# Feed-forward up and gate products by 2x2 blocks with seven block products in six of eight row pairs, activations stationary

## The chip, the cores and the metric

One core of one Trainium2 chip runs the kernel: one launch, 256 tokens, two layers. The metric is the device time of that launch in microseconds. The engines are named as the profile names them: PE (matrix products; PEld is its weight load), DVE (vector), ACT (scalar, activations), POOL (GpSimd), SP (which issues most of the DMAs). Tensors lie in HBM; the engines work on SBUF, and PE writes its sums to the eight banks of PSUM, each 128 partitions by 512 float32.

## The reference

Two layers on x of 256 x 2048, all in float32. Each has mixers (a recurrence and pooling in the first, linear and sparse attention in the second), an output projection, and a feed-forward part. Only the feed-forward parts are touched:

```python
D_MODEL = 2048
D_FF = 4 * D_MODEL                                  # 8192
D_FF_2 = -(-8 * D_MODEL // (3 * 256)) * 256         # 5632
...
h2 = rms_norm(x, mlp_norm[i])
x = x + jnp.square(jax.nn.relu(h2 @ w_ffn_up[i])) @ w_ffn_down[i]
...
m = rms_norm_2(h, ffn_norm_g)
return h + (jax.nn.silu(m @ w_gate) * (m @ w_up)) @ w_down
```

## The kernel before

**Products.** A float32 operand is split in two tiles of a shorter format (fp32r): a high part (a rounding, by ACT) and a low part (the operand less its high part, by DVE). A product is three matmuls: high by high, high by low, low by high. Weights are split as they arrive: `load` (L231) brings 512 KB into a tile `r` (128 x 1024; the pool `raw` has 5), `stream` (L236) makes `h` with ACT at L240 and `l` with DVE at L244 (the pools `hi` and `lo` have 3 each).

**Two forms of product.** `gemm_a` (L251) holds 128 x 128 of the weights stationary and moves the 256 tokens: 16 blocks of K (the summed dimension) by three matmuls of 256 columns (L262 to L264) give one tile of 128 outputs by 256 tokens. `gemm_b_part` (L725) holds 128 x 128 of the activations stationary and moves 512 columns of weights (L740 to L742).

**Feed-forward 1** (in `block1`, L820): eight rounds. A round has an up stage (eight `gemm_a` tiles, 1024 of the 8192 hidden columns, each followed by ReLU, a square and a split) and a down stage (four column blocks of `gemm_b_part` over the round's 1024 hidden rows, added into x by DVE). **Feed-forward 2** (`ffn2`, L1331): six rounds of the same kind with a gate tile and an up tile for each 128 of the 5632 hidden columns. In all that is 64 + 88 tiles of `gemm_a`, or 19 lots of eight, and a lot covers 1024 weight columns over the whole K of 2048.

**What sets the order.** The code is written in program order. A scheduler, working from its own estimate of durations, then fixes one order of instructions per engine at compile time, and allocates each pool's slots. At run time each engine follows its order strictly, waiting on semaphores for inputs and for slots to come free. PSUM has three pools: `acc` (4 banks), `fr` (2), `ch` (2).

## Time and profile before

| | |
|---|---|
| device time, median of 3 runs | 2485.89 us (2485.54 to 2486.83) |
| span of the profiled execution, first to last instruction | 2485.7 us |
| PE busy | 2455.0 us, 99% |
| DVE busy | 1547.7 us, 62% |
| ACT busy | 1149.9 us, 46% |
| POOL busy | 217.5 us, 9% |
| mean granted PE clock, as a share of full speed | 0.993 |

The table is the profile's first part. Matmuls are pipelined: the duration of one record overlaps the next, so PE's rate is read from the distance between starts. A share over the whole span mixes stages, so the windows and timelines of single stages, below, are what the argument rests on.

### The profile page before, as it was taken

How to read it: one execution, taken by the hardware profiler on the slowest of the kernel's cores; microseconds unless marked ns; L12 is line 12 of the kernel's file. 1: busy time of each engine (PE TensorE's matmuls, PEld its weight loads, DVE VectorE, ACT ScalarE, POOL GpSimd, SP SyncE). 2: the span in 40 equal slices, each digit the busy share in tenths (PEclk: the TensorE clock that was granted, in tenths of full speed). 3: DMA queues.
4: the chain of work that ended last, by engine and by line, in shares of the span. 5: the costliest groups of instructions: out<-in, count | busy, mean ns of one | idle time of the engine just before them, and what ended most of it. 6: DMA issues, size and time to landing. Idle time of an engine off the chain costs nothing.

```text
span 2485.7 us, 40916 instructions
## 1 busy us (share of the span) xinstructions
PE 2455.0 (99%) x16396; PEld 2224.1 (89%) x16396; DVE 1547.7 (62%) x2436; ACT 1149.9 (46%) x1686; POOL 217.5 (9%) x321
## 2 busy tenths in 40 slices
PE   9999999999999999999999998999999999999999
PEld 8988888989989989988887897888989999998988
DVE  7788866555555555556674677766555555555555
ACT  5545445544444444445652466545444444444443
POOL 1543320000000000000010044200000000000000
PEclk9999999999999999999999999999999999999999
DMA  6443336555555555556556543255555655555554
GB/s 230 153 130 111 97 115 237 182 192 186 187 190 185 188 192 187 187 189 235 180 184 213 179 149 118 90 196 185 179 190 185 187 186 186 188 185 187 186 190 158
DMA packets 135406, 439.59 MB, mean 177 GB/s; under 512 B 26784, under 2 KB 29216, under 8 KB 134064
## 3 DMA queue, kind: packets, MB, share of 16 engines
q1 hardware_dynamic: 130032, 423.58, 52.1%
q10 hardware_dynamic: 5184, 13.41, 1.4%
q8 instruction: 128, 2.10, 0.3%
q14 instruction: 62, 0.51, 0.1%
HBM read 429.59 MB, written 7.34 MB: 176 GB/s over the span
## 4 chain that ended last, share of the span: by engine, by line
PE 94%; DVE 4%; ACT 1%; DMA 1%; issue 1%; POOL 0%; SPq 0%; DVEq 0%; ACTq 0%
PE acc L262 16%; PE acc L263 16%; PE acc L264 16%; PE acc L740 13%; PE acc L741 13%; PE acc L742 13%; PE ch L361 3%; PE fr L361 2%; DVE l L244 1%; PE fr L782 1%; PE acc L361 1%; PE ch L582 0%; PE ch L585 0%; DVE X L1002 0%; PE acc L375 0%
## 5 line engine op out<-in xcount | busy, mean ns | idle before, releaser
L244 DVE TENSOR_TENSOR l<-r,h 128x1024 fp32r<-128x1024 f32 x774 | 951.5, 1230 | 737.0 <-ACT h L240 728.8
L240 ACT CAST h<-r 128x1024 fp32r<-128x1024 f32 x780 | 818.8, 1050 | 1102.2 <-PE acc L742 448.1
L262 PE MATMUL acc<-qh,h 128*128 128x256 f32 x1824 | 520.8, 286 | 0.0
L264 PE MATMUL acc<-qh,l 128*128 128x256 f32 x1824 | 519.3, 285 | 0.0
L263 PE MATMUL acc<-ql,h 128*128 128x256 f32 x1824 | 519.2, 285 | 0.0
L264 PE MATMUL acc<-xh,l 128*128 128x256 f32 x1536 | 439.0, 286 | 0.5 <-DVE l L244 0.5
L262 PE MATMUL acc<-xh,h 128*128 128x256 f32 x1536 | 439.4, 286 | 0.0
L263 PE MATMUL acc<-xl,h 128*128 128x256 f32 x1536 | 438.6, 286 | 0.0
L262 PEld LDWEIGHTS acc<-qh,h 128*128 128x128 f32 x1824 | 350.5, 192 | 4.0 <-issue 3.5
L263 PEld LDWEIGHTS acc<-ql,h 128*128 128x128 f32 x1824 | 350.5, 192 | 1.7 <-issue 1.2
L264 PEld LDWEIGHTS acc<-qh,l 128*128 128x128 f32 x1824 | 350.2, 192 | 1.1 <-issue 0.9
L741 PE MATMUL acc<-l,qh 128*128 128x512 f32 x768 | 300.4, 391 | 0.0
L742 PE MATMUL acc<-h,ql 128*128 128x512 f32 x768 | 299.3, 390 | 0.0
L263 PEld LDWEIGHTS acc<-xl,h 128*128 128x128 f32 x1536 | 295.8, 193 | 2.7 <-issue 1.3
L262 PEld LDWEIGHTS acc<-xh,h 128*128 128x128 f32 x1536 | 295.6, 193 | 2.8 <-issue 0.9
L264 PEld LDWEIGHTS acc<-xh,l 128*128 128x128 f32 x1536 | 295.7, 193 | 2.5 <-DVE l L244 0.7
L740 PE MATMUL acc<-h,qh 128*128 128x512 f32 x768 | 275.2, 392 | 0.0
L741 PE MATMUL acc<-l,xh 128*128 128x512 f32 x608 | 237.2, 390 | 0.0
L742 PE MATMUL acc<-h,xl 128*128 128x512 f32 x608 | 236.3, 389 | 0.0
L740 PE MATMUL acc<-h,xh 128*128 128x512 f32 x608 | 214.7, 390 | 0.0
L740 PEld LDWEIGHTS acc<-h,qh 128*128 128x128 f32 x768 | 144.0, 188 | 30.8 <-issue 1.2
L741 PEld LDWEIGHTS acc<-l,qh 128*128 128x128 f32 x768 | 144.2, 188 | 29.9 <-issue 0.4
(413 smaller groups left out, 2418.4 us busy)
## 6 DMA issues: line engine op xcount, KB each, us to landing
r<-w_ffn_up SPq DMA_DIRECT2D x128, 512.0 KB, 3.3
r<-w_ffn_down SPq DMA_DIRECT2D x128, 512.0 KB, 3.4
r<-w_gate SPq DMA_DIRECT2D x88, 512.0 KB, 3.9
r<-w_up SPq DMA_DIRECT2D x88, 512.0 KB, 3.5
r<-w_down SPq DMA_DIRECT2D x88, 512.0 KB, 4.2
r<-w_in SPq DMA_DIRECT2D x70, 512.0 KB, 3.4
r<-w_out SPq DMA_DIRECT2D x64, 512.0 KB, 3.3
r<-w_in_2a SPq DMA_DIRECT2D x58, 512.0 KB, 3.3
```

The costliest lines, as they stand in the source:

```text
L240: nc.scalar.copy(h, r)
L244: eng.tensor_sub(l, r, h.bitcast(F32))
L262: nc.tensor.matmul(o, wh, xh, start=k == 0, stop=False)
L263: nc.tensor.matmul(o, wh, xl, start=False, stop=False)
L264: nc.tensor.matmul(o, wl, xh, start=False, stop=k == n - 1)
L361: self.nc.tensor.matmul(out, lhsT, rhs, start=start, stop=stop)
L740: nc.tensor.matmul(ps[t], ah, wh, start=first and k == 0, stop=False)
L741: nc.tensor.matmul(ps[t], ah, wl, start=False, stop=False)
L742: nc.tensor.matmul(ps[t], al, wh, start=False, stop=last and k == nk - 1)
L782: nc.tensor.transpose(ps[:, o:o + 128], self.x[:, t, kk * 128:kk * 128 + 128], self.c("ident"))
```

## The change

The up and gate products no longer use `gemm_a`. A new method `group` computes 256 tokens by 1024 columns with activations stationary, and there are 8 + 11 = 19 groups, one for each lot above; in the second feed-forward part a group holds 512 gate and 512 up columns side by side. K is taken in eight row pairs of 256. A pair of rows times 1024 columns is a 2x2 problem: token halves by K blocks by column halves. Pairs 0 and 4 (`PLAIN`) make it with eight block products, the other six with seven, in Winograd's form of Strassen's scheme. A block product is three matmuls of 512 columns.

The seven products need sums of the weight blocks. Two tiles carry them: `t13` (two of the sums, made by one DVE addition) and `t24` (two more, made by two POOL additions, the second from the first). `t13`, `t24` and two plain pieces (`ra`, and the first half of `rb`) are each split into high and low. The low parts are made by DVE (`ra`, `t13`), by POOL (half of `rb`; the second half of `t24`), and the first half of `t24` by POOL in odd pairs and by DVE in even ones. A pool `more` (2 slots each) holds the parts of `rb` and `t24`, a pool `sums` (2) the sums. The sums of activations are made once, in `pair_chunk`, which takes the place of `norm_chunk` ahead of both feed-forward parts. All eight PSUM banks belong to one pool during the feed-forward parts; a group accumulates seven or eight products in eight banks over all pairs and then combines them (three ACT copies, eight DVE additions). The results have tokens on partitions, so they are transposed back by PE (`to_hidden`) for the down products. Down stages keep their matmuls (`ffn_down`). They run one round late: group 1 follows group 0 without a down stage between in the first part, and in the second part groups 1, 2, 3, 5, 7 and 9 follow a group directly.

```diff
+PLAIN = (0, 4)
...
-    a["w_ffn_up"] = lay_a(g["w_ffn_up"][0], 64)
+    a["w_ffn_up"] = lay_s(g["w_ffn_up"][0])
...
-    a["w_gate_2"] = lay_a(g["w_gate_2"][0], 44)
-    a["w_up_2"] = lay_a(g["w_up_2"][0], 44)
+    both = np.stack([g["w_gate_2"][0].reshape(D, 11, 512), g["w_up_2"][0].reshape(D, 11, 512)], 2)
+    a["w_gu_2"] = lay_s(both.reshape(D, 11 * 1024))
...
+            a12, a22, s1, s3, s2, s4, a11, a21 = (f[:, j] for j in range(8))
+            nc.vector.tensor_sub(s1, a21, a22)
+            nc.gpsimd.tensor_sub(s3, a11, a21)
+            nc.vector.tensor_sub(s2, s1, a11)
+            nc.vector.tensor_add(s4, a12, s2)
+            nc.scalar.copy(h, f[:, :7])
+            nc.vector.tensor_sub(l, f[:, :7], h.bitcast(F32))
...
+    def lows(self, r, h, eng=None):
+        l = self.low(r.shape[-1], r.shape[-1] < 1024)
+        (eng or self.nc.vector).tensor_sub(l, r, h.bitcast(F32))
+        return l
+    def low(self, n=1024, more=False):
+        return (self.more if more else self.lo).tile([128, 1024], F32R, name="l", tag="l")[:, :n]
+    def highs(self, r, more=False):
+        h = (self.more if more else self.hi).tile([128, 1024], F32R, name="h", tag="h")[:, :r.shape[-1]]
+        self.nc.scalar.copy(h, r)
+        return h
+    def three(self, ps, a, h, l, w, first, last):
+        mm = self.nc.tensor.matmul
+        ah, al = a
+        mm(ps, ah, h[:, w], start=first, stop=False)
+        mm(ps, ah, l[:, w], start=False, stop=False)
+        mm(ps, al, h[:, w], start=False, stop=last)
...
+    def group(self, w, pairs, out):
+        nc = self.nc
+        q = {}
+        turn = self.hold()
+        one, two = slice(0, 512), slice(512, 1024)
+        def add(name, a, h, l, w, first, last):
+            if first:
+                q[name] = self.bank("acc")
+            self.three(q[name], a, h, l, w, first, last)
+        start = min(i for i in range(8) if i not in PLAIN)
+        for i in range(8):
+            sh, sl = pairs[i]
+            a = [(sh[:, j], sl[:, j]) for j in range(sh.shape[1])]
+            ra = self.load(w[i, 0].rearrange("p k n -> p (k n)"))
+            rb = self.load(w[i, 1].rearrange("p k n -> p (k n)"))
+            if i in PLAIN:
+                ha = self.highs(ra)
+                la = self.lows(ra, ha)
+                hb = self.highs(rb)
+                lb = self.lows(rb, hb)
+                f = i == PLAIN[0]
+                add("8", a[1], hb, lb, two, f, False)
+                add("8", a[3], ha, la, two, False, i == PLAIN[-1])
+                add("2", a[0], ha, la, one, f, False)
+                add("2", a[2], hb, lb, one, False, False)
+                add("3", a[0], hb, lb, two, f, False)
+                add("3", a[2], ha, la, two, False, False)
+                add("4", a[1], ha, la, one, f, False)
+                add("4", a[3], hb, lb, one, False, False)
+                if i == 0:
+                    turn()
+                continue
+            a12, a22, s1, s3, s2, s4, a11 = a
+            f, e = i == start, i == 7
+            t13 = self.sums.tile([128, 1024], F32, name="t13", tag="t")
+            nc.vector.tensor_add(t13.rearrange("p (a n) -> p a n", a=2), ra.rearrange("p (a n) -> p a n", a=2),
+                                 rb[:, two].unsqueeze(1).to_broadcast([128, 2, 512]))
+            t24 = self.sums.tile([128, 1024], F32, name="t24", tag="t")
+            nc.gpsimd.tensor_add(t24[:, one], t13[:, one], ra[:, two])
+            nc.gpsimd.tensor_add(t24[:, two], t24[:, one], rb[:, one])
+            h = self.highs(ra)
+            l = self.lows(ra, h)
+            add("1", a11, h, l, one, f, e)
+            add("3", s4, h, l, two, False, e)
+            h = self.highs(rb[:, one], True)
+            l = self.lows(rb[:, one], h, nc.gpsimd)
+            add("2", a12, h, l, one, False, e)
+            h = self.highs(t13)
+            l = self.lows(t13, h)
+            add("5", s1, h, l, one, f, e)
+            add("7", s3, h, l, two, f, e)
+            h = self.highs(t24, True)
+            l = self.low(more=True)
+            (nc.gpsimd if i % 2 else nc.vector).tensor_sub(l[:, one], t24[:, one], h[:, one].bitcast(F32))
+            nc.gpsimd.tensor_sub(l[:, two], t24[:, two], h[:, two].bitcast(F32))
+            add("6", s2, h, l, one, f, e)
+            add("4", a22, h, l, two, False, e)
+        c11, c12, c21, c22 = out
+        V = nc.vector
+        tmp = lambda: self.comb.tile([128, 512], F32, name="cb", tag="cb")
+        c1, u2, u3 = tmp(), tmp(), tmp()
+        nc.scalar.copy(c22, q["8"])
+        nc.scalar.copy(c1, q["1"])
+        nc.scalar.copy(c12, q["3"])
+        V.tensor_add(c11, c1, q["2"])
+        V.tensor_add(c12, c12, q["5"])
+        V.tensor_add(c22, c22, q["5"])
+        V.tensor_add(u2, c1, q["6"])
+        V.tensor_add(u3, u2, q["7"])
+        V.tensor_add(c21, u3, q["4"])
+        V.tensor_sub(c12, c12, u2)
+        V.tensor_sub(c22, c22, u3)
...
+    def to_hidden(self, cols, hidden, j0, banks):
+        nc = self.nc
+        for k in range(0, 4, 2):
+            ps = banks[k // 2]
+            for a in range(2):
+                for t in range(2):
+                    o = a * 256 + t * 128
+                    nc.tensor.transpose(ps[:, o:o + 128], cols[t][:, (k + a) * 128:(k + a) * 128 + 128], self.c("ident"))
+            hh, hl = (x[(j0 + k) // 4][:, (j0 + k) % 4:(j0 + k) % 4 + 2].rearrange("p k t -> p (k t)") for x in hidden)
+            nc.scalar.copy(hh, ps)
+            nc.vector.tensor_sub(hl, ps, hh.bitcast(F32))
...
-        for s in range(8):
-            hh, hl = self.half_tiles()
-            for i in range(8):
-                ps = self.gemm_a(I["w_ffn_up"], s * 8 + i, act)
-                a = tp.tile([128, T], F32, name="relu", tag="relu")
-                nc.scalar.activation(a, ps, AF.Relu)
-                b = tp.tile([128, T], F32, name="relu2", tag="relu2")
-                nc.vector.tensor_mul(b, a, a)
-                self.split(hh[i], hl[i], b)
...
+        for s in range(9):
+            if s < 8:
+                c = [tp.tile([128, 512], F32, name="c", tag="c", bufs=4) for _ in range(4)]
+                self.group(I["w_ffn_up"][s], self.n_pairs, c)
+                hidden = self.hidden_quarts()
+                for n in range(2):
+                    for t in range(2):
+                        x = c[2 * t + n]
+                        nc.scalar.activation(x, x, AF.Relu)
+                        nc.scalar.activation(x, x, AF.Square)
+                    self.later.append(((c[n], c[2 + n]), hidden, 4 * n))
+                ready.append(hidden)
+            if s == 0:
...
+    def ffn_down(self, w, hidden, s, add, then=None, nk=8):
+        chunks = [(h[:, k], l[:, k]) for h, l in zip(*hidden) for k in range(4)][:nk]
+        for n in range(4):
+            ps = self.acc2()
+            turn = self.hold()
+            self.gemm_b_part(ps, w, n, chunks, s * 8, True, True)
+            turn()
+            add(n, ps)
...
-        for s in range(6):
-            nh = 8 if s < 5 else 4
-            hh, hl = (x[s % 2 * 8:s % 2 * 8 + nh] for x in hidden)
-            for i in range(nh):
-                j = s * 8 + i
-                g = tp.tile([128, T], F32, name="g", tag="g")
-                nc.vector.tensor_mul(g, self.gemm_a(I["w_gate_2"], j, act), rb)
-                nc.scalar.activation(g, g, AF.Silu)
-                u = tp.tile([128, T], F32, name="u", tag="u")
-                nc.vector.tensor_mul(u, self.gemm_a(I["w_up_2"], j, act), rb)
-                nc.vector.tensor_mul(u, u, g)
-                self.split(hh[i], hl[i], u)
...
+        for g in range(12):
+            if g < 11:
+                c = [tp.tile([128, 512], F32, name="c", tag="c", bufs=4) for _ in range(4)]
+                self.group(I["w_gu_2"][g], self.n_pairs, c)
+                if g % 2 == 0:
+                    hidden = self.hidden_big(g // 2)
+                    ready.append(hidden)
+                for t in range(2):
+                    gate, up = c[2 * t:2 * t + 2]
+                    nc.scalar.activation(gate, gate, AF.Silu, scale=r[:, t:t + 1])
+                    nc.vector.scalar_tensor_tensor(gate, up, r[:, t:t + 1], gate, ALU.mult, ALU.mult)
+                self.later.append(((c[0], c[2]), hidden, g % 2 * 4))
+            if g % 2 and g > 1 and g < 11:
+                self.ffn_down(I["w_down_2"], ready.pop(0), g // 2 - 1, self.add_x)
+        self.ffn_down(I["w_down_2"], ready.pop(0), 4, self.add_x)
+        self.ffn_down(I["w_down_2"], ready.pop(0), 5, store, nk=4)
```

How the orders change. On DVE, first a row of an up stage of the kernel before (`l` is the low part of a weight tile `r`; `relu2` a hidden tile, `ql` its low part):

```order
L244 TENSOR_TENSOR l_5994<-r_5990,h_5992 128x1024
L842 TENSOR_TENSOR relu2_5918<-relu_5916 128x256
L244 TENSOR_TENSOR l_6024<-r_6020,h_6022 128x1024
L249 TENSOR_TENSOR ql_5651<-relu2_5918,qh_5650 128x256
L244 TENSOR_TENSOR l_6061<-r_6057,h_6059 128x1024
L842 TENSOR_TENSOR relu2_5985<-relu_5983 128x256
L244 TENSOR_TENSOR l_6091<-r_6087,h_6089 128x1024
L249 TENSOR_TENSOR ql_5653<-relu2_5985,qh_5652 128x256
L244 TENSOR_TENSOR l_6128<-r_6124,h_6126 128x1024
L842 TENSOR_TENSOR relu2_6052<-relu_6050 128x256
```

and then pairs 5, 6 and 7 of a group of the changed kernel (`t13`, and the low parts `l` of `r` and of `t13`; one row makes half of the low part of a `t24`):

```order
L910 TENSOR_TENSOR t13_7108<-r_7104,r_7106 128x1024
L853 TENSOR_TENSOR l_7115<-r_7104,h_7113 128x1024
L853 TENSOR_TENSOR l_7132<-t13_7108,h_7130 128x1024
L910 TENSOR_TENSOR t13_7155<-r_7151,r_7153 128x1024
L853 TENSOR_TENSOR l_7162<-r_7151,h_7160 128x1024
L853 TENSOR_TENSOR l_7179<-t13_7155,h_7177 128x1024
L853 TENSOR_TENSOR l_7209<-r_7198,h_7207 128x1024
L910 TENSOR_TENSOR t13_7202<-r_7198,r_7200 128x1024
L928 TENSOR_TENSOR l_7189<-t24_7157,h_7187 128x512
L853 TENSOR_TENSOR l_7226<-t13_7202,h_7224 128x1024
```

Between two activation tiles DVE had two subtractions of 1024 columns for 128 output columns; now every pair of rows has an addition and two subtractions of 1024, and none of the activation's.

On POOL, before, around the first feed-forward part (the last rows of the first mixer, L902 at the end of the first layer, L1187 in the second):

```order
L651 TENSOR_TENSOR pd_4912<-pf_4914,u_4897 128x16
L620 TENSOR_TENSOR y_4131<-y_4131,bv_2811 128x256
L620 TENSOR_TENSOR y_4145<-y_4145,bv_3113 128x256
L902 TENSOR_TENSOR x_res_5089<-x_res_5089,fn_12519 128x2048 x2
L1187 MEMSET cu_15003 128x3
```

and in the changed kernel pairs 5 and 6 of the same group:

```order
L853 TENSOR_TENSOR l_7125<-r_7106,h_7123 128x512
L913 TENSOR_TENSOR t24_7110<-t13_7108,r_7104 128x512
L914 TENSOR_TENSOR t24_7110<-t24_7110,r_7106 128x512
L928 TENSOR_TENSOR l_7142<-t24_7110,h_7140 128x512
L929 TENSOR_TENSOR l_7142<-t24_7110,h_7140 128x512
L853 TENSOR_TENSOR l_7172<-r_7153,h_7170 128x512
L913 TENSOR_TENSOR t24_7157<-t13_7155,r_7151 128x512
L914 TENSOR_TENSOR t24_7157<-t24_7157,r_7153 128x512
L929 TENSOR_TENSOR l_7189<-t24_7157,h_7187 128x512
```

POOL had no instruction in the feed-forward part; it now has four or five of 512 columns in each pair of seven products, and the two that end a pair wait for ACT's rounding of `t24`.

On DVE at the passage from a down stage to a group (the first row is the last weight tile of the down stage, `x_res` its additions, then the group's pairs 0 and 1):

```order
L267 TENSOR_TENSOR l_7587<-r_7583,h_7585 128x1024
L910 TENSOR_TENSOR t13_7651<-r_7647,r_7649 128x1024
L853 TENSOR_TENSOR l_7613<-r_7607,h_7611 128x1024
L853 TENSOR_TENSOR l_7617<-r_7609,h_7615 128x1024
L1022 SCALAR_TENSOR_TENSOR x_res_5105<-acc_7527,r2_5720,x_res_5105 128x512
L1022 SCALAR_TENSOR_TENSOR x_res_5105<-acc_7528,r2_5720,x_res_5105 128x512
L853 TENSOR_TENSOR l_7658<-r_7647,h_7656 128x1024
L910 TENSOR_TENSOR t13_7702<-r_7698,r_7700 128x1024
L853 TENSOR_TENSOR l_7676<-t13_7651,h_7674 128x1024
```

The `t13` of pair 1 stands ahead of the two subtractions of pair 0, and both stand ahead of the down stage's last additions.

## Rows read from the trace of the kernel before

**Rows 1.** The page, part 1: busy time (share of the span) x instructions of each engine.

```profile
PE 2455.0 (99%) x16396; PEld 2224.1 (89%) x16396; DVE 1547.7 (62%) x2436; ACT 1149.9 (46%) x1686; POOL 217.5 (9%) x321
```

**Rows 2.** The page, part 4: the chain that ended last, by engine and line.

```profile
PE 94%; DVE 4%; ACT 1%; DMA 1%; issue 1%; POOL 0%; SPq 0%; DVEq 0%; ACTq 0%
PE acc L262 16%; PE acc L263 16%; PE acc L264 16%; PE acc L740 13%; PE acc L741 13%; PE acc L742 13%; PE ch L361 3%; PE fr L361 2%; DVE l L244 1%; PE fr L782 1%; PE acc L361 1%; PE ch L582 0%; PE ch L585 0%; DVE X L1002 0%; PE acc L375 0%
```

**Rows 3.** Windows over two up stages and the down stage between; columns in the second line.

```profile
core 0 of [0], span 2485.7 us
core 0: us, PE busy (x) PEld busy (x) DVE busy (x) ACT busy (x) POOL busy (x), PEclk, DMA share, GB/s
918.00:964.00 46.00, 46.00 (x385) 46.00 (x384) 25.35 (x32) 20.89 (x30) 0.00 (x0) 1.00 0.57 184
964.00:1007.50 43.50, 43.50 (x194) 36.03 (x193) 24.38 (x25) 17.45 (x18) 0.00 (x0) 1.00 0.61 193
1007.50:1053.50 46.00, 46.00 (x384) 45.96 (x384) 25.46 (x32) 20.88 (x30) 0.00 (x0) 1.00 0.56 184
```

**Rows 4.** Timeline of PE where a down stage passes into an up stage.

```profile
start us, us, engine line op out<-in xcount [idle before <-releaser]
...
917.26 0.39 PE L740 MATMUL acc<-h,qh 128*128 128x512 f32 x1
917.49 0.39 PE L741 MATMUL acc<-l,qh 128*128 128x512 f32 x1
917.72 0.39 PE L742 MATMUL acc<-h,ql 128*128 128x512 f32 x1
917.94 0.28 PE L262 MATMUL acc<-xh,h 128*128 128x256 f32 x1
918.06 0.28 PE L263 MATMUL acc<-xl,h 128*128 128x256 f32 x1
918.18 0.28 PE L264 MATMUL acc<-xh,l 128*128 128x256 f32 x1
```

**Rows 5.** Timeline of PE, six transposes between two matmuls of the out projection.

```profile
417.06 0.82 PE L782 MATMUL fr<-cst,x_res 128*128 128x128 f32 x6
...
417.63 0.48 PE L741 MATMUL acc<-l,qh 128*128 128x512 f32 x1
```

**Rows 6.** Groups by line: busy us, mean ns, idle before. First DVE, then ACT, then POOL.

```profile
L244 DVE TENSOR_TENSOR l<-r,h 128x1024 fp32r<-128x1024 f32 x774 | 951.5, 1230 | 737.0 <-ACT h L240 728.8 <-PE fr L361 0.5
L240 ACT CAST h<-r 128x1024 fp32r<-128x1024 f32 x780 | 818.8, 1050 | 1102.2 <-PE acc L742 448.1 <-PE acc L263 347.6 <-issue 261.6
...
L812 DVE TENSOR_TENSOR x_res<-x_res,acc 128x512 f32<-128x512 f32 x64 | 41.0, 680 | 6.2 <-PE acc L742 6.2
...
L491 POOL TENSOR_TENSOR G<-G,cst 128x512 f32<-128x512 f32 x12 | 15.6, 1302 | 14.9 <-ACT G L490 14.9
L244 POOL TENSOR_TENSOR l<-r,h 128x1024 fp32r<-128x1024 f32 x6 | 14.4, 2403 | 33.9 <-ACT h L240 31.3 <-ACT rhs L577 2.6
...
L1253 POOL TENSOR_TENSOR E<-b 128x512 f32<-128x512 f32 x7 | 8.6, 1241 | 19.7 <-DVE b L1231 7.1 <-PE fr L361 6.3 <-PE acc L264 3.3
```

**Rows 7.** Single lines, min/median/max ns: POOL L354, and DVE L1260 (both inputs in SBUF).

```profile
L354 POOL TENSOR_TENSOR d<-z x27: 612/613/1593, 38.6 to 249.3; 128x256 f32<-128x256 f32 x27
...
L1260 DVE TENSOR_TENSOR E<-E,Q x7: 673/681/1219, 1547.3 to 1586.2; 128x512 f32<-128x512 f32 x7
```

**Rows 8.** Timeline of POOL and DVE from 90 us: start us, us, engine, line.

```profile
89.54 0.73 POOL L472 TENSOR_TENSOR BKh<-sig,cum 128x256 f32<-128x256 f32 x1 [0.57 <-DVE sig L469]
...
89.71 0.41 DVE L352 TENSOR_TENSOR z<-acc,rb 128x256 f32<-128x256 f32 x1
...
90.23 0.74 POOL L475 TENSOR_TENSOR BKe<-sig,e_end 128x256 f32<-128x256 f32 x1
...
90.38 1.67 DVE L244 TENSOR_TENSOR l<-r,h 128x1024 fp32r<-128x1024 f32 x1
...
90.93 1.59 POOL L354 TENSOR_TENSOR d<-z 128x256 f32<-128x256 f32 x1
```

**Rows 9.** Timeline of DVE and POOL from 157 us.

```profile
157.63 1.22 DVE L244 TENSOR_TENSOR l<-r,h 128x1024 fp32r<-128x1024 f32 x1
...
157.76 2.25 POOL L491 TENSOR_TENSOR ql<-ql,cst 128x512 f32<-128x512 f32 x1 [1.09 <-ACT ql L490]
```

**Rows 10.** Windows in the recurrence and the second mixer, with the granted clock (PEclk).

```profile
159.80:163.20 3.40, 1.58 (x14) 1.39 (x13) 1.11 (x3) 0.82 (x2) 1.29 (x3) 1.00 0.67 164
163.20:166.60 3.40, 1.90 (x20) 1.84 (x21) 2.05 (x4) 0.36 (x1) 1.05 (x4) 0.67 0.89 206
1542.20:1545.60 3.40, 3.40 (x31) 3.40 (x30) 3.40 (x6) 3.01 (x5) 3.32 (x4) 1.00 0.02 5
1545.60:1549.00 3.40, 0.66 (x6) 0.48 (x5) 3.40 (x6) 2.23 (x3) 3.28 (x4) 1.00 0.46 157
1549.00:1552.40 3.40, 2.17 (x16) 1.87 (x14) 3.40 (x7) 2.41 (x10) 1.30 (x2) 0.67 0.00 0
```

More of the change, by code (lines that the diff above doesn't have):

```diff
@@ L364, in first_tiles @@
         nc = self.nc
-        out = [self.acc.tile([128, 512], F32, name="acc", tag="acc")[:, :T] for _ in range(n)]
+        out = [self.bank("acc")[:, :T] for _ in range(n)]
         for half in range(2):
@@ new lines, in hold, with turn @@
+    def hold(self):
+        todo, self.later = [(x, [self.bank("fr") for _ in range(2)]) for x in self.later], []
+        def turn():
+            for x, banks in todo:
+                self.to_hidden(*x, banks)
+        return turn
+    def to_hidden(self, cols, hidden, j0, banks):
+        nc = self.nc
+        for k in range(0, 4, 2):
[7 more added lines that the diff above has]
+            nc.vector.tensor_sub(hl, ps, hh.bitcast(F32))
@@ L1234, in gla_scores @@
         sc = [scA[:, :, :128], scB]
-        ps = [self.fr.tile([128, 512], F32, name="fr", tag="fr") for _ in range(2)]
+        ps = [self.bank("fr") for _ in range(2)]
         for t in range(2):
```

237 lines of the change are left out of this document (158 added, 79 removed).

## The prediction, made before the changed kernel ran

> **What bounds the kernel now.** Read the page first: PE is busy 99% of the span, DVE 62%, ACT 46%, POOL 9% [rows 1]. Then the chain that ended last: 94% of it is PE, nearly all in the two product forms [rows 2]. Then one up stage alone: for 46 us PE never stops, while DVE works 25.35, ACT 20.89 and POOL nothing [rows 3]. So the up and gate products are bound by PE's own rate, and a saving there counts in full as long as the engines that feed PE keep up. Whether they do is the question here.
>
> PE's rate is read from starts [rows 4]: 512 columns every 0.227 us (917.26, 917.49, 917.72), 256 columns every 0.120 us. A lot of eight tiles is 384 matmuls of 256 columns, 384 x 0.120 = 46.1 us, which is the window of [rows 3]; the 19 lots take 876 us. A down stage is 192 x 0.227 = 43.5 us and is not changed.
>
> **What the change takes from PE.** The order of the built kernel has 3306 matmuls of 512 columns in the groups, 174 in each: 2 pairs x 24 + 6 x 21. 174 x 0.227 = 39.4 us, 6.6 less than 46.1, and 19 x 6.64 = 126 us in all. So the change does what it says, and a version that lacks the saving is no rival. Against it stand 216 transposes. Six of them and the next matmul are 0.57 us apart [rows 5], 0.095 each. 152 of them lie in down stages, where PE is the bound: +14 us. The other 64 lie at the start of a group, where I expect PE to wait anyway: nothing, and 6 us if that cover is gone.
>
> **What it puts on DVE and POOL.** Counts are from the built order, over all 19 groups. DVE: 114 additions for t13 and 304 subtractions, 418 of 1024 columns, each with both inputs in SBUF, at 1.23 us [rows 6]; 98 of 512 columns with both inputs in SBUF (half low parts, the last two of the combination, the gate product) at 0.68 us [rows 7]; and six additions a group with one input in PSUM, also 0.68 [rows 6]. POOL: 532 operations of 512 columns, where it had none. A lone one takes 1.24 to 1.30 us, half of the one of 1024 columns with the fp32r output is 1.20 [rows 6]; I take 1.25. For one group that is DVE 22 x 1.23 + 5.2 x 0.68 = 30.6 us and POOL 28 x 1.25 = 35.0 us. Side by side either would fit under PE's 39.4.
>
> **They don't run side by side.** This is the reading on which all rests. In [rows 8] POOL's L475 starts at 90.23 and DVE's subtraction L244 at 90.38. L244 takes 1.67 us in place of 1.23: it stands until POOL is through at 90.97. POOL's next one, L354 (128x256, 0.61 us when alone, its median in [rows 7]), starts at 90.93 and takes 1.59: it stands until DVE is through at 92.05. In [rows 9] the roles are the other way: DVE starts first, takes its 1.22, and POOL's 512-column operation takes 2.25, 1.0 more than alone. L352, which reads PSUM, runs through POOL's L472 at its usual 0.41 [rows 8]. So a DVE operation with two inputs in SBUF and a POOL operation wait for each other, and those of DVE in a group are of just that kind: L244 is the very operation that the new low parts are, and t13 has two SBUF inputs as well. What is saved at a change of hands: the three of [rows 8] take 92.52 - 90.23 = 2.29 us where 0.74 + 1.23 + 0.61 = 2.58 would be the sum, so 0.14 for each of two changes.
>
> The Trainium skill has this as a rule: on "SBUF — State Buffer", section "Who interferes with whom", a DVE instruction with two SBUF inputs and a GpSimd instruction that reads SBUF exclude each other, and the later one blocks until the other has finished. The trace agrees but for the 0.14 us. By the page alone there would be no saving at the change of hands, and the low end of the sum below would be 2750 in place of 2617.
>
> **The sum for a group.** Both engines share one door, so their times add: 30.6 + 35.0 = 65.6 us a group. At best there is a saving at both ends of each of the 27 DVE operations, 27 x 2 x 0.14 = 7.6: 58.0. At worst the door is empty while POOL waits in each of six pairs for ACT to round t24 (L240's 1.05 us [rows 6]) and DVE has nothing ready: 65.6 + 6.3 = 71.9. I take 65.6, the two set against each other, since DVE's order has the next pair's work behind each of its rows but the slots (3 in lo, 2 in sums) hold it back some of the time. All three are above the 46.1 of before, so in the groups PE waits for low parts and sums; its 39.4 us lie beside them and no longer count.
>
> How much of a group's work is done before PE reaches it? During a down stage the door is half empty (DVE 24.38 of 43.5 us, POOL 0 [rows 3]). By the order and the slots, the two low parts of pair 0, the t13 of pair 1 and POOL's five operations of pair 1 can be done ahead: 3 x 1.23 + 5 x 1.25 = 9.95 us; then lo, sums and more are full. At a group's end PE still has six matmuls behind the last low part (1.4 us), while two subtractions of the combination (1.4) are not waited for: these cancel. So:
>
> - 7 groups follow a group directly: 65.6 - 46.1 = +19.5 each, +137.
> - 12 follow a down stage or an out projection: 55.6 - 46.1 = +9.5 each, +114.
> - transposes in down stages: +14.
> - where a group ends, the next stage's first two banks wait for an ACT copy and a DVE addition (0.68 [rows 6]) that stand behind low parts in DVE's order: 0 to 2 us, 1 taken, x 19 = +19.
> - PE's clock: in the groups PE works 39.4 of 55.6 to 65.6 us, 60 to 71%. In [rows 10] a window with 1.58 us busy of 3.40 is followed by one at 0.67 of the full clock, and one with 0.66 likewise; windows with 3.40 busy are not. At half speed (1.2 GHz) a pair's 21 matmuls would take twice 4.76, 9.5 us, still about what the door takes for it, so a fall is covered but where it reaches into the next stage: up to 3.4 us at half speed, 1.7 lost, x 19 = 32. I take 10.
>
> Sum: 2485.7 (the span; the median of the runs is 2485.89, the same to 0.2 us) + 137 + 114 + 14 + 19 + 10 = 2780. With 58.0 for a group: 7 x 11.9 + 12 x 2.8 + 14 = 131, 2617. With 71.9 (11 us of it ahead): 7 x 25.8 + 12 x 14.8 + 14 + 38 + 32 = 443, 2929.
>
> Costed at nothing: ACT's roundings, 22 x 1.05 + 6 of half the size, about 26 us, and under 12 us of copies and activations, in 55 to 66 us; the loads, 1 MB a pair in 9 us and more, where before it was 1 MB in 5.8 us at a DMA share of 0.57 [rows 3]; the sums of activations, 24 small operations of DVE and POOL for each feed-forward part, beside the out projection.
>
> **The rivals.**
>
> 1. *PE stays the bound, and the kernel is faster.* If the new forms do not exclude each other (t13's second input is read twice over, POOL's outputs are partly fp32r), POOL's 35.0 us plus six waits of 1.05 are 41 us a group, about PE's 39.4 plus transposes. Then the time is 2485.7 - 126 + 20 + 19 = 2399. It turns on the door's time for a group, g: 7 x (g - 46.1) + 12 x (g - 56.1) + 43 is nothing at g = 50 us, and below that the kernel is faster. Against it: in [rows 8] and [rows 9] the engines exclude each other in both directions with the same kind of operands.
>
> 2. *The door stands empty in the waits.* The two engines pass work back and forth: t13 (DVE), two additions (POOL), rounding (ACT), low parts (POOL). If DVE's strict order has nothing ready in each of these waits, the group is at 71.9 or somewhat over and the time at 2870 to 2960. For it: two slots in sums. Against it: DVE's three operations of the next pair.
>
> 3. *PE's clock stays at 1.2 GHz in the groups.* Then PE's 174 matmuls take twice 39.4, 79 us a group, PE is the bound again, and the time is 2485.7 + 19 x 32.7 + 33 = 3140. For it: [rows 10]. [...]
>
> **How the numbers follow.** The door as bound, in its own range 2617 to 2929, has 0.88, of which the upper part from 2870 (rival 2) has 0.18; rival 1 has 0.07; rival 3 has 0.04; 0.01 is left for a time within 0.2% of before, where the gain and the door's cost happen to meet. The forecast is 2780. The range of 2630 to 2930 leaves out rivals 1 and 3 and the edges. A change of 0.2% is about what a measurement of this kernel can tell from none; faster 0.07, same 0.01, slower 0.92.
>
> **What would show it.** In the changed kernel's trace: in the groups PE idle, waiting for low parts from POOL and DVE; L853, L913 and L929 on POOL at about 2.3 us where DVE works beside them, and the 1024-column operations of DVE at 1.7 to 2.4; DVE and POOL never both moving; a group of 55 to 66 us by windows, a down stage still at 43.5 to 45. I am wrong if POOL's operations stay near 1.25 us while DVE is busy (rival 1), if the granted clock in the groups is near 0.5 (rival 3), or if DVE and POOL both stand idle a good part of a group (rival 2).

## The result, and the profile after

The changed kernel takes 2790.24 us (median of 4 runs, 2785.5 to 2791.44), the kernel before 2486.34 us in the same comparison: a ratio of 1.1215, 95% interval 1.1199 to 1.1231. That is 304 us slower, inside the range and 10 us from the forecast. The profiled execution spans 2789.4 us.

The page of after, part 1 (compare [rows 1]), and the PE clock in 40 slices:

```profile
PE 2520.0 (90%) x12618; PEld 2041.0 (73%) x12618; DVE 2052.6 (74%) x2548; ACT 1362.7 (49%) x1915; POOL 1241.4 (45%) x865
...
PEclk9999999899999999999999999998889989898999
```

PE has 3778 fewer instructions and is no longer busy all the time; POOL has gone from 217.5 to 1241.4 us. Its added records take 1028 us: 532 operations, 1.93 us each, where a lone one of this size takes 1.24 to 1.30 [rows 6].

Groups by line, DVE then POOL (busy us, mean ns of one | idle before it):

```profile
L853 DVE TENSOR_TENSOR l<-r,h 128x1024 fp32r<-128x1024 f32 x190 | 367.6, 1945 | 29.6 <-ACT h L861 28.8
L853 DVE TENSOR_TENSOR l<-t,h 128x1024 fp32r<-128x1024 f32 x114 | 200.7, 1760 | 122.7 <-ACT h L861 122.7
L910 DVE TENSOR_TENSOR t<-r 128x1024 f32<-128x1024 f32 x114 | 194.1, 1703 | 62.1 <-POOL t L913 28.5 <-POOL l L929 13.1 <-DMA r<-w_ffn_up 10.9
...
L913 POOL TENSOR_TENSOR t<-t,r 128x512 f32<-128x512 f32 x114 | 242.8, 2130 | 51.5 <-DVE l L853 46.0 <-POOL l L929 4.1
L914 POOL TENSOR_TENSOR t<-t,r 128x512 f32<-128x512 f32 x114 | 240.5, 2109 | 6.5
L853 POOL TENSOR_TENSOR l<-r,h 128x512 fp32r<-128x512 f32 x114 | 215.3, 1889 | 398.3 <-ACT h L861 398.3
```

DVE's operations of 1024 columns with two SBUF inputs, 1.23 us before [rows 6], take 1.70 to 1.95 now. The timelines of POOL and DVE in one group show the two taking turns (start us, us):

```profile
2180.77 2.16 POOL L913 TENSOR_TENSOR t<-t,r 128x512 f32<-128x512 f32 x1
2182.88 2.26 POOL L853 TENSOR_TENSOR l<-r,h 128x512 fp32r<-128x512 f32 x1
2185.10 2.27 POOL L914 TENSOR_TENSOR t<-t,r 128x512 f32<-128x512 f32 x1
2188.53 2.20 POOL L928 TENSOR_TENSOR l<-t,h 128x512 fp32r<-128x512 f32 x1 [1.16 <-ACT h L861]
2190.69 1.29 POOL L929 TENSOR_TENSOR l<-t,h 128x512 fp32r<-128x512 f32 x1
2191.95 1.29 POOL L853 TENSOR_TENSOR l<-r,h 128x512 fp32r<-128x512 f32 x1
...
2179.80 1.98 DVE L853 TENSOR_TENSOR l<-t,h 128x1024 fp32r<-128x1024 f32 x1 [0.26 <-ACT h L861]
2181.70 4.52 DVE L853 TENSOR_TENSOR l<-r,h 128x1024 fp32r<-128x1024 f32 x2
2186.47 1.98 DVE L910 TENSOR_TENSOR t<-r 128x1024 f32<-128x1024 f32 x1 [0.25 <-DMA r<-w_gu]
2188.37 1.21 DVE L853 TENSOR_TENSOR l<-r,h 128x1024 fp32r<-128x1024 f32 x1
```

While DVE is at work, POOL's operations take 2.16 to 2.27; once DVE has stopped, at 2189.58, the next two take 1.29 each. DVE's pair of 4.52 us is 2.26 each. Read by where the records end, one operation ends at a time and nothing is lost between them: DVE's pair ends at 2186.22, POOL's L914 at 2187.37 (1.15 later), DVE's L910 at 2188.45 (1.08 later). So a record of 2.2 us is some 1.1 us of waiting for the other engine and some 1.1 us of work. This is [rows 8, 9] for a whole group.

Windows: a group behind a down stage and the down stage after it, then two groups that follow a group directly (columns in the first line):

```profile
core 0: us, PE busy (x) PEld busy (x) DVE busy (x) ACT busy (x) POOL busy (x), PEclk, DMA share, GB/s
647.25:698.80 51.55, 41.53 (x164) 31.00 (x163) 37.63 (x25) 25.19 (x29) 43.05 (x23) 0.95 0.42 141
698.80:747.65 48.85, 48.85 (x221) 40.32 (x220) 37.13 (x37) 24.54 (x30) 12.57 (x8) 0.99 0.60 195
...
1982.60:2045.30 62.70, 50.44 (x183) 36.08 (x182) 55.40 (x37) 29.23 (x37) 50.32 (x29) 0.85 0.41 134
2045.30:2107.90 62.60, 50.50 (x184) 35.71 (x183) 55.12 (x37) 29.08 (x36) 50.08 (x29) 0.88 0.41 135
```

The borders of the last two are the marks at which ACT fetches one product of a group from PSUM (L938). Just 36 DVE and 28 POOL operations start between two such marks, the operations of exactly one group: 62.7 us, where an up stage took 46.0 [rows 3]. The other five groups that follow a group are 68.3 to 69.1 us apart by the same marks. In their windows 38 DVE and 30 POOL operations start: the last ones of the group before lie behind its mark, about 4.4 us by their lone times. By their records DVE and POOL are "busy" 55 and 50 us of each 62.7, more than that together: the excess is waiting for each other. From the timelines of both, at least one of them has a record in 61.0 of the 62.7 us, so the two stand idle together for only 1.7.

Where the 304 us are, by the first matmul of each stretch in both traces (the third stretch up to the end of its last matmul, the last to the end of the program's):

| stretch | before | after | more | in the sum? |
|---|---|---|---|---|
| out projection 1, to the first group | 126.8 | 136.8 | +10.0 | no |
| feed-forward 1, first seven groups and six down stages | 584.7 | 673.2 | +88.5 | yes |
| its last group, two down stages, gate stage behind | 226.8 | 251.4 | +24.6 | 11 of it |
| from there to out projection 2 | 363.3 | 368.1 | +4.8 | no |
| out projection 2, to the first group | 90.0 | 96.7 | +6.7 | no |
| feed-forward 2 | 747.8 | 917.0 | +169.1 | yes |

So some 269 us lie in the groups and their down stages, and 35 at the passages into and out of the feed-forward parts, which the sum did not have.

### The profile page after: what moved, and what is told of

Its sections match the earlier page's. It is cut to its first block, busy times and chain, and to the rows that moved or that the text cites. A ratio compares the mean times of both kernels' runs of the same rounds, so it can differ in the third digit from the quotient of the medians.

```text
span 2789.4 us, 34680 instructions
## 1 busy us (share of the span) xinstructions
PE 2520.0 (90%) x12618; PEld 2041.0 (73%) x12618; DVE 2052.6 (74%) x2548; ACT 1362.7 (49%) x1915; POOL 1241.4 (45%) x865
## 3 DMA queue, kind: packets, MB, share of 16 engines
q8 instruction: 99, 1.62, 0.2%
## 5 line engine op out<-in xcount | busy, mean ns | idle before, releaser
L263 ACT CAST h<-r 128x1024 fp32r<-128x1024 f32 x476 | 498.5, 1050 | 545.1 <-PE acc L769 370.5
L861 ACT CAST h<-t 128x1024 fp32r<-128x1024 f32 x228 | 237.0, 1047 | 420.8 <-POOL t L914 249.1
L853 POOL TENSOR_TENSOR l<-r,h 128x512 fp32r<-128x512 f32 x114 | 215.3, 1889 | 398.3 <-ACT h L861 398.3
L861 ACT CAST h<-r 128x1024 fp32r<-128x1024 f32 (+1 forms) x304 | 262.1, 886 | 113.2 <-PE acc L870 78.4
L853 DVE TENSOR_TENSOR l<-t,h 128x1024 fp32r<-128x1024 f32 x114 | 200.7, 1760 | 122.7 <-ACT h L861 122.7
L868 PE MATMUL acc<-h,sh 128*128 128x512 f32 x570 | 214.8, 441 | 57.6 <-ACT h L861 52.8
L913 POOL TENSOR_TENSOR t<-t,r 128x512 f32<-128x512 f32 x114 | 242.8, 2130 | 51.5 <-DVE l L853 46.0
L869 PE MATMUL acc<-l,sh 128*128 128x512 f32 x570 | 249.4, 437 | 17.2 <-DVE l L853 14.0
L914 POOL TENSOR_TENSOR t<-t,r 128x512 f32<-128x512 f32 x114 | 240.5, 2109 | 6.5
L929 POOL TENSOR_TENSOR l<-t,h 128x512 fp32r<-128x512 f32 x114 | 208.5, 1829 | 75.1 <-ACT h L861 61.3
L870 PE MATMUL acc<-h,sl 128*128 128x512 f32 x570 | 241.2, 423 | 0.0
L910 DVE TENSOR_TENSOR t<-r 128x1024 f32<-128x1024 f32 x114 | 194.1, 1703 | 62.1 <-POOL t L913 28.5
```

Source lines behind the costliest of these rows:

```text
L263: nc.scalar.copy(h, r)
L853: (eng or self.nc.vector).tensor_sub(l, r, h.bitcast(F32))
L861: self.nc.scalar.copy(h, r)
L868: mm(ps, ah, h[:, w], start=first, stop=False)
L869: mm(ps, ah, l[:, w], start=False, stop=False)
L870: mm(ps, al, h[:, w], start=False, stop=last)
```

## Experiments: is it the door?

**One-input operations on DVE.** POOL and the roundings stay, and so does who waits for whom, but for two things: t13 no longer waits for rb, and the low parts no longer read r. DVE's two-input operations of 1024 columns become one-input ones; every call of `lows` on DVE becomes one of `lows1`.

```diff
+        self.nc.vector.tensor_scalar(l, h.bitcast(F32), 2.0 ** -13, 0.0, ALU.mult, ALU.add)
...
-            nc.vector.tensor_add(t13.rearrange("p (a n) -> p a n", a=2), ra.rearrange("p (a n) -> p a n", a=2),
-                                 rb[:, two].unsqueeze(1).to_broadcast([128, 2, 512]))
+            nc.vector.tensor_scalar(t13, ra, 1.0, 0.25, ALU.mult, ALU.add)
...
-            l = self.lows(t13, h)
+            l = self.lows1(t13, h)
```

> DVE's two-input operations of 1024 columns in the groups become operations with one SBUF input of the same width (t13 is ra plus a constant, low parts are the high part times 2^-13), so the product isn't the reference's: the sum with rb and the subtraction of r are left out. POOL's operations, their inputs, the roundings of ACT and who waits for whom stay. Theory A: if it is the two SBUF inputs that shut POOL out, POOL's 512-column ops fall from 2.3 to 1.25 us, a group comes to POOL's 35 us plus waits or PE's 39.4, and the time to 2486 - 126 + 14 + 19 + 33 = about 2430, below the kernel before. Theory C, the group is a chain of waits between four engines (t13, two sums, rounding, low part): the chain is the same, only DVE's links are shorter (six of perhaps 1.2 to 0.6 us), so a group falls from 62.7 by at most 6 us, the time to 2680 or more. If one-input operations shut POOL out too, POOL's ops stay at 1.25 plus DVE's time, and the time lies between, by how long DVE's one-input op is.

Measured: 2589.87 us, ratio 1.0406 (1.0391 to 1.0422). The third outcome: one-input operations shut POOL out too. Its timeline, three DVE operations, then POOL: one alone, three with DVE beside them.

```profile
2207.58 0.68 DVE L874 TENSOR_SCALAR l<-h 128x1024 fp32r<-128x1024 f32 x1
2208.77 1.19 DVE L874 TENSOR_SCALAR l<-h 128x1024 fp32r<-128x1024 f32 x1 [0.52 <-ACT h L861]
2209.89 1.78 DVE L915 TENSOR_SCALAR t<-r 128x1024 f32<-128x1024 f32 x1
...
2201.65 1.29 POOL L918 TENSOR_TENSOR t<-t,r 128x512 f32<-128x512 f32 x1
...
2207.79 1.62 POOL L917 TENSOR_TENSOR t<-t,r 128x512 f32<-128x512 f32 x1 [0.68 <-POOL l L933]
2209.36 1.75 POOL L853 TENSOR_TENSOR l<-r,h 128x512 fp32r<-128x512 f32 x1
2211.08 1.73 POOL L918 TENSOR_TENSOR t<-t,r 128x512 f32<-128x512 f32 x1
```

1024 columns by one input take 0.68 us when undisturbed, about half of 1.23, but 1.19 and 1.78 behind a POOL operation, and POOL's 1.29 becomes 1.62 to 1.75. By durations a group is then 22 x 0.68 + 5.2 x 0.68 + 28 x 1.25 = 53.5 us. The marks of a group behind a group are 53.0 to 55.1 us apart. The chain of waits alone (theory C) allowed a fall of 6 us a group and a total of 2680 or more. The two groups of 62.7 us fall by 8 to 9 us, the other five by 15 to 16, and the total falls by 200. The Trainium skill has this too ("SBUF — State Buffer", section "Who interferes with whom"): operations such as `tensor_scalar`, which can run in a two-port mode, can contend for the shared ports as well. The trace agrees: half the time (0.68 us for 1.22), and POOL still waits.

**POOL writes and doesn't read.**

```diff
-            nc.gpsimd.tensor_add(t24[:, one], t13[:, one], ra[:, two])
-            nc.gpsimd.tensor_add(t24[:, two], t24[:, one], rb[:, one])
+            nc.gpsimd.memset(t24[:, one], 0.5)
+            nc.gpsimd.memset(t24[:, two], 0.5)
...
```

> POOL's operations of the groups become memsets of the same tiles: POOL writes as much but reads nothing, so t24's sums and the low parts that POOL made are left out; the waits of POOL on DVE's t13 and on ACT's roundings go as well. Theory A: a POOL operation that doesn't read SBUF doesn't shut DVE out; DVE's 1024-column ops are back at 1.23 us, DVE has 31 us a group, and PE is the bound at 39.4: about 2430. If writing is enough to shut out, DVE's ops stay above 1.5 us and a group is about 31 plus 28 memsets. Theory D, that what holds a group is PE's clock (granted 0.83 to 0.90 there): the groups keep that clock and stay over 46 us.

Measured: 2440.01 us, ratio 0.9804 (0.9789 to 0.9819). Groups by line:

```profile
L853 DVE TENSOR_TENSOR l<-r,h 128x1024 fp32r<-128x1024 f32 x190 | 230.1, 1221 | 24.9 <-ACT h L861 24.9
L910 DVE TENSOR_TENSOR t<-r 128x1024 f32<-128x1024 f32 x114 | 139.4, 1223 | 53.0 <-DMA r<-w_gu 22.9 <-DMA r<-w_ffn_up 16.1 <-ACT h L861 13.4
...
L913 POOL MEMSET t<- 128x512 f32 x114 | 60.1, 527 | 70.2 <-DVE l L932 41.0 <-DVE l L853 21.3 <-ACT h L861 7.3
```

DVE is back at 1.22 us with POOL busy beside it, and the groups are PE's. This run takes waits away together with the reads, so by itself it doesn't part the door from the chain; it shows that PE at 174 matmuls a group is nearly as cheap as worked out, 85.9 us for a group and its down stage where 84.6 was worked out with the transposes. The low clock of after's groups (theory D) goes with the waits: without them it is 1.00 in the same window.

```profile
692.10:778.00 85.90, 85.90 (x384) 70.53 (x383) 59.55 (x60) 49.92 (x59) 13.88 (x28) 1.00 0.58 197
```

**All of POOL's work on DVE.**

```diff
-            nc.gpsimd.tensor_add(t24[:, one], t13[:, one], ra[:, two])
-            nc.gpsimd.tensor_add(t24[:, two], t24[:, one], rb[:, one])
+            nc.vector.tensor_add(t24[:, one], t13[:, one], ra[:, two])
+            nc.vector.tensor_add(t24[:, two], t24[:, one], rb[:, one])
...
-            l = self.lows(rb[:, one], h, nc.gpsimd)
+            l = self.lows(rb[:, one], h)
...
```

> All of POOL's work in the groups (t24's two additions, the low part of half of rb, t24's low part) goes to DVE; POOL is empty there. Theory A, the shared door: only the sum of the two engines' times counts, and DVE does in 0.68 us what POOL does in 1.25. DVE a group: 4 x 1.23 (plain pairs) + 6 x (4 x 1.23 + 3 x 0.68) + 8 x 0.68 + about 2 = 54 us, in place of the 62.7 us that a group takes after a group. So 7 x (54 + 1 - 46.1) = 62, 12 groups after a down stage +2.5 each with the 11 us still ahead = 30, transposes 14, and the 33 us that the changed kernel lost around the out projections and in the gate stage behind the feed-forward: 2486 + 139 = about 2625, 165 us faster than the changed kernel. Rival B, the engines work beside each other and the longer of the two sets the group (POOL's 35 us of ops, each of them slow by itself at 2.3 us, 60 us): DVE's 54 us is then also the end, 2625 as well, but in it DVE's ops would stay at the 1.9 us mean that the changed kernel shows, 22 x 1.9 and more, over 60 us and no gain. Told apart by DVE's mean time of a 1024-column op: A 1.23, B 1.9.

Measured: 2547.39 us, ratio 1.0236 (1.0219 to 1.0252), 243 us below the changed kernel. One engine with all the work beats two that share it. Groups by line, then windows of a group behind a group and of the next group with its down stage:

```profile
L853 DVE TENSOR_TENSOR l<-t,h 128x1024 fp32r<-128x1024 f32 x114 | 139.4, 1222 | 23.3 <-ACT h L861 23.1
L910 DVE TENSOR_TENSOR t<-r 128x1024 f32<-128x1024 f32 x114 | 139.2, 1221 | 8.1 <-DMA r<-w_ffn_up 4.4 <-DMA r<-w_gu 3.7
```

```profile
2048.90:2102.10 53.20, 46.12 (x183) 33.94 (x182) 50.47 (x59) 29.03 (x37) 0.00 (x0) 0.94 0.48 159
2102.10:2189.30 87.20, 85.98 (x375) 69.06 (x374) 74.40 (x83) 45.59 (x52) 0.00 (x0) 1.00 0.58 192
```

DVE's operations are at 1.22, as A said. A group behind a group takes 53.2 us with DVE busy 50.5 of it. The estimate of 2625 was 78 us high: behind a down stage a group costs no more than PE takes, since DVE, with no POOL to wait for, finishes its share in the down stage's gaps (88.4 us for group and down stage, 89.6 before).

**Twelve of POOL's 28 operations on DVE.** The two additions for t24 alone are moved.

> Of POOL's 28 operations a group in the changed kernel the 12 additions for t24 go to DVE, 16 stay. Theory A: the door's time falls by 12 x (1.25 - 0.68) = 6.8 us a group, DVE 38.8 plus POOL 20.0, 58.8 us where 65.6 was worked out and 62.7 seen for a group behind a group: about 56 now, and a group with its down stage about 94 in place of 101. In all 2790 - 19 x 6.8 = about 2660, on a line between the changed kernel and the one with all of it on DVE (2547). If the engines worked beside each other, POOL's 20 and DVE's 43 us would both fit in PE's 40 or nearly, and the time would be under 2550.

Measured: 2659.99 us, ratio 1.0693 (1.068 to 1.0707), with 2660 expected. Windows of two groups that follow a group:

```profile
1912.40:1971.30 58.90, 48.76 (x182) 35.15 (x182) 55.30 (x49) 29.08 (x36) 30.56 (x17) 0.91 0.43 143
1971.30:2030.40 59.10, 48.37 (x182) 34.72 (x182) 55.61 (x49) 29.20 (x37) 30.20 (x17) 0.91 0.42 142
```

DVE's and POOL's lone times for a group, added up, against the groups that follow a group (all seven by their marks; for the changed kernel the two with one group's operations between the marks):

| kernel | DVE + POOL | sum | measured |
|---|---|---|---|
| changed | 30.6 + 35.0 | 65.6 | 62.7 |
| t24's sums on DVE | 38.8 + 20.0 | 58.8 | 58.2 to 59.7 |
| one-input operations | 18.5 + 35.0 | 53.5 | 53.0 to 55.1 |
| all on DVE (here with its six additions from PSUM, 4.1) | 52.9 + 0 | 52.9 | 53.1 to 53.3 |

In the three kernels in which both engines work, with quite different shares, the sum gives the time within 3 us; the larger of the two does not.

## Experiments: waits and passages

**A third slot for t13 and t24**, in the second feed-forward.

```diff
-self.sums = self.pool("sums", 2, es=es)
+self.sums = self.pool("sums", 3, es=es)
```

> The changed kernel with three slots in place of two for t13 and t24, in the second feed-forward alone (there is no room for it in the first); six of the seven groups that follow a group lie there. Theory A, the door is held nearly all the time: a third slot lets an addition start earlier, but not the sum of times shrink; groups stay within 1 us of 62.7, the time within 10 us of 2790. Rival 2, the door stands empty in the waits of the chain t13, t24, rounding, low part: a third slot lets the next pair's sums go ahead, and a group loses up to the 6 us of roundings, 11 groups some 30 to 60 us: 2730 to 2760.

Measured: 2756.15 us, ratio 1.1078 (1.1063 to 1.1093): 34 us less, in the range that rival 2 named. The two groups of 62.7 us are now 61.3 and 60.9:

```profile
1976.00:2037.30 61.30, 49.55 (x184) 35.85 (x183) 53.81 (x37) 29.88 (x36) 51.68 (x29) 0.89 0.42 138
2037.30:2098.20 60.90, 49.00 (x181) 35.31 (x180) 55.68 (x37) 29.63 (x36) 52.58 (x29) 0.89 0.42 138
```

In these two the time in which neither DVE nor POOL has a record falls from 1.7 us to 0.6 and 0.3, most of what they gain. Two groups with their down stage take 158.6 to 159.8 where the changed kernel takes 167, and in such a pair the time without a record falls from some 19.3 us to 12.5 to 13.7. So the door did stand empty, for 1.7 us in a group by itself and for longer beside a down stage, and this kernel fills most of the first and part of the second. The scheduler also set a new order for this kernel (181 of POOL's 865 instructions stand at another place), and the slot and the order were not parted.

**The banks left as they are.** The changed kernel closes PSUM's three pools ahead of each feed-forward part and makes one ring of eight of them; here they stay.

```diff
+BANK = {"8": "acc", "3": "acc", "2": "ch", "4": "ch", "1": "acc", "5": "acc", "6": "fr", "7": "fr"}
...
-                q[name] = self.bank("acc")
+                q[name] = self.bank(BANK[name])
...
-        self.banks({"acc": 8})
...
-        self.banks({"acc": 4, "fr": 2, "ch": 2})
...
-        self.banks({"acc": 8})
```

> The changed kernel, with the eight banks left as they are through the whole program (results 8, 3, 1 and 5 in the four banks of the row results, 2 and 4 in two, 6 and 7 in those of the transposes). If setting up the banks anew cost the 10.0 and 6.7 us around the out projections and some 12 behind the first feed-forward, the time falls by 25 to 30 us, to about 2763, with the groups as slow as before. If the loss is the queue of ACT and DVE ahead of the first group, it stays at 2790.

Measured: 2728.21 us, ratio 1.0964 (1.0947 to 1.0981), 62 us less, twice what was expected. Windows at the end of out projection 1 and over the last down stages with the gate stage, first of after, then of this kernel:

```profile
470.80:479.00 8.20, 2.22 (x9) 1.50 (x9) 4.97 (x8) 6.02 (x12) 6.27 (x5) 0.74 0.65 236
1216.20:1403.50 187.30, 178.98 (x802) 145.67 (x801) 114.89 (x145) 97.77 (x146) 0.00 (x0) 0.98 0.55 189
```

```profile
469.30:479.00 9.70, 9.70 (x48) 7.81 (x46) 6.22 (x15) 8.00 (x15) 5.21 (x3) 1.00 0.57 201
1203.90:1377.80 173.90, 173.90 (x805) 144.44 (x804) 113.61 (x144) 96.96 (x146) 0.00 (x0) 1.00 0.60 203
```

With new banks PE stands almost idle from the last matmul of the out projection until the last pairs have been transposed and fetched; with the old ones it goes straight on into the first group. Stretch by stretch, from first matmul to first matmul, the passages are 8.4, 13.4, 6.9 and 6.7 us shorter, 35 in all, which is what the table above has outside the groups. The rest comes off inside the groups and their down stages: 2.6 us in feed-forward 1 and 19 in feed-forward 2, by the trace of the longest of the four runs. Which of the bank assignments does that was not tried, and the order of instructions changed with them.

**Both repairs.**

> Both repairs of the changed kernel at once, six pairs of seven products kept: POOL's work in the groups on DVE (which alone gave 2790 to 2547) and the banks left as they are (which alone gave 2790 to 2728, some 35 us of it at the passages to and from the feed-forward parts, the rest in the groups). If the two are separate causes, the 35 us at the passages come off 2547 as well and the groups stay bound by DVE's own 53 us where a group follows a group: 2505 to 2515, still above the kernel before, since 7 groups then cost 53.2 + 1 in place of 46.2. If the bank gain in the groups adds too: 2485 to 2500. If the banks only mattered because POOL's and DVE's work was late: 2535 or more.

Measured: 2505.55 us, ratio 1.0065 (1.0048 to 1.0082): the first outcome, with two separate causes. Of 62 us the banks give 42 here. What is left is DVE, as the window of 50 us inside two groups shows (DVE 49.87):

```profile
2000.00:2050.00 50.00, 44.30 (x178) 31.20 (x177) 49.87 (x59) 29.47 (x35) 0.00 (x0) 1.00 0.50 164
```

**New banks, but earlier**, before the out projection (with three pairs of seven products, as in the next section).

> The three-pair kernel with all on DVE and one ring of eight banks (2496 us), with the banks set up anew before the out projection begins and set back before the feed-forward's last down stage. If the loss there was the setting up while the last pairs' transposes still hold banks: the 9.4, 6.7 and about 9 us are gone, 2496 - 25 = about 2471, and down to 2465 since its groups with their down stages were 1 to 2 us shorter than those with fixed banks (87.6 against 89.6). If the out projection now waits for its own banks, it is 2480 or more.

Measured: 2498.11 us, ratio 1.0045 (1.0032 to 1.0057), no gain on 2496. From the last matmul of out projection 1 to the first group it is 3.5 us where it was 9.0, and the passage behind feed-forward 1 is 10 us shorter, but out projection 1 takes 152.8 us up to its last matmul where it took 128.7. The cost moves with the place at which the pools are closed.

## Experiments: how many pairs are worth it

With all on DVE, three pairs of seven products, and one ring of eight banks:

> Three pairs of seven products in place of six (pairs 2, 4 and 7), the others plain, and all on DVE. PE: 5 x 24 + 3 x 21 = 183 matmuls, 41.5 us a group. DVE, by theory A with no POOL in the way: 10 x 1.23 + 3 x 6.96 + 8 x 0.68 + 1.5 = 40 us, just under PE. So PE bounds the groups: 2486 - 19 x 4.6 + 14 (transposes) + 19 (group ends) + 33 (as seen around the out projections and behind the feed-forward) = about 2465, a little faster than the kernel before. If the chain of waits (C) sets the time, three chains a group cost as before, some 8 us each: over 2560.

Measured: 2496.32 us, ratio 1.003 (1.0019 to 1.0041), 31 us above what was expected. By its first matmuls the groups and their down stages are some 18 us shorter than before, the passages some 30 longer, and so PE's saving is lost there. With the banks left as they are, zero, three and two pairs:

> The stationary activations alone: all eight pairs take eight block products, no sums of weights, no seven products; POOL has no work in the groups. The eight banks are not set up anew for the feed-forward parts (4 for products and row results, 2 for transposes, 2 more, as in the kernel before), since four results need only four banks. PE 192 x 0.227 = 43.6 us a group against 46.24, 19 x 2.65 = 50 us saved; 216 transposes x 0.095 = 21 us more, as all of them lie beside a busy PE now; 0 to 1 us at each group's end. If the loss around the out projections (10.0 and 6.7 us in the changed kernel) and behind the feed-forward comes of setting up the banks anew, it is gone: 2486 - 50 + 21 + 10 = about 2467. If it comes of the pairs themselves (the copies and roundings for the last pairs), it stays and the time is about 2490, that of before.

> The kernel of three pairs of seven products, all on DVE (pairs 2, 4 and 6 here), with the banks left as they were before the feed-forward: results 8, 3, 1 and 5 take the four banks of the row results, 2 and 4 two, 6 and 7 those of the transposes. The three-pair kernel with new banks lost 9.4 and 6.7 us around the out projections and about 9 behind the first feed-forward, and gained 18 in the feed-forward parts. If the new banks are the cause of the loss: 2496 - 25 = about 2471, faster than before. If not, 2496 again.

> As the one before with two pairs of seven products (3 and 6). PE 186 x 0.227 = 42.2 us a group, DVE 27.8 + 2 x 4.5 = 36.8 us, 5 us under PE, so DVE has room also where a group follows a group: 2486 - 19 x 4.0 + 21 + 19 = about 2450 if PE is the bound throughout; 2470 if waits at the ends of groups grow with each combination.

| pairs of seven products, on DVE, banks kept | us | ratio to before (95%) |
|---|---|---|
| none | 2479.74 | 0.9962 (0.9950 to 0.9975) |
| two | 2470.91 | 0.9937 (0.9924 to 0.9949) |
| three | 2475.11 | 0.9950 (0.9938 to 0.9962) |
| six | 2505.55 | 1.0065 (1.0048 to 1.0082) |

All but the last beat both kernels, by less than 1% but with intervals that leave out 1. The three-pair kernel gains some 20 us by its banks (2496 to 2475, with 2471 expected); another choice of third pair and another order of two products changed with them. Stationary activations alone give 7 us, where 19 was expected: two groups and a down stage take 134.2 us for 135.7, but one group and a down stage 89.6 as before. Two pairs give 9 us more, of the 26 that PE saves in them. In the windows of a group behind a down stage and of the down stage behind it, with two pairs, PE is busy nearly without a gap by its records, so what is left there is PE's own time.

```profile
693.30:737.00 43.70, 43.19 (x188) 34.97 (x187) 28.85 (x30) 20.23 (x23) 0.00 (x0) 1.00 0.60 191
736.90:782.60 45.70, 45.67 (x210) 37.64 (x209) 30.66 (x34) 23.64 (x29) 0.00 (x0) 1.00 0.55 186
```

Two and three pairs can't be told apart by their intervals; what keeps the third from paying was not followed further. With six, DVE is the bound where a group follows a group (49.87 of 50 us, above).

## Why the prediction was right, and where its sum was off

- **PE saves 6.6 us a group**: right within some 1.5 us. With POOL out of the door's way the time falls under that of before (2440 us, clock 1.00).
- **The door**: right, and the heart of it. The added times of DVE and POOL, not the larger, set a group, over three shares of the work. Rival 1 (beside each other, 2399) falls with it.
- **One sign came out only in part**: PE was to wait for low parts. It waits 82.2 us for those of DVE and POOL, but 105.1 us for ACT's roundings (L861). ACT itself waits 249.1 us for POOL's second addition (L914) before it rounds sums, so the door lies behind those waits too.
- **65.6 us a group**: a little too large; one group's operations take 62.7. Two things were to cancel, the saving at a change of hands and the empty door. The saving can be read from the ends of the records: behind a POOL operation a DVE one of 1024 columns ends 1.08 us later (1.22 alone), behind a DVE operation a POOL one ends 1.15 later (1.25 alone). With 47 changes of hand in such a group that is some 6 us of the 7.6 named. The door is empty for 1.7 us of the 6.3 named. Together that gives some 61.3; the last 1.4 us was not followed.
- **7 groups at +19.5, 12 at +9.5**, with transposes and ends: two groups and a down stage in feed-forward 2 took 167.0 us for 135.7 (+31.3, worked out as some +33), one group and a down stage 101.0 for 89.6 (+11.35, some +12), four groups and one +65.9 (some +75). In all about 269 where the sum has 294: some 9 of these 25 us lie in the first four groups of feed-forward 2, the rest is 1 to 2 us at each of the others.
- **9.95 us done ahead**: wrong in the picture, though group and down stage together are about as long as worked out. In the down stage that begins at 698.80 POOL works 9 us on the last pairs of the group before, then nothing for 35 us, and takes up the next group only 4 us ahead of PE (747.65), as the timeline of POOL has it:

```profile
706.19 2.29 POOL L929 TENSOR_TENSOR l<-t,h 128x512 fp32r<-128x512 f32 x1
743.43 1.74 POOL L853 TENSOR_TENSOR l<-r,h 128x512 fp32r<-128x512 f32 x1 [34.95 <-ACT h L861]
745.13 2.28 POOL L913 TENSOR_TENSOR t<-t,r 128x512 f32<-128x512 f32 x1
```

  So it is the tail of a group, more than the head, that lies beside the down stage, and the window of the down stage, with 12 of the group's matmuls in it, takes 48.9 us rather than 43.5 to 45.
- **Clock, 10 us**: granted 0.85 to 0.95 in the windows of groups above, so rival 3 (1.2 GHz, 0.5) falls. In the ten down stages directly behind a group the shortfall of the granted clock (the length of the window times one less PEclk) comes to 0 to 1.8 us each, 10.8 in all. The 10 was picked below a bound of 32 without a working, so that it meets the 10.8 is luck.
- **Rival 2**: a share of it is true, not as a time of 2870 but as 1.7 us inside the 62.7.
- **What the sum lacked**: the passages, 35 us. The prediction counted the first group as one behind a down stage and costed the transposes there at nothing. It did not see that pools closed and opened anew hold up PE at either end of each feed-forward part. That 25 too many in the groups and 35 left out come to 10 is luck; the mechanism isn't.

## What to carry to other kernels

Where POOL reads SBUF beside DVE operations like these, with two SBUF inputs or in the one-input form of 0.68 us for 1024 columns, add the two engines' times up; an operation then belongs where it is shorter, and here 0.68 us on a busy DVE was worth more than 1.25 on an idle POOL. A saving on PE counts only down to the next engine's time in the same stage, so take as many of the cheaper products as that engine can feed (two or three pairs here, not six). When PSUM pools are laid out anew between stages, look for the gap on PE at that place.
